# The 32 sample rows copied into all four partition quadrants, and their hi/lo products stacked into one full-array matmul

## The chip, the cores and the metric

The kernel runs on one core of a Trainium2 chip. The metric is the device time of one execution in microseconds (us). TensorE multiplies; ScalarE and VectorE read its results and prepare its operands; SyncE issues all DMAs.

## The reference

Two layers (DEPTH) are applied to two token streams at once: a prompt of 256 rows and a sample of 32 rows, both of 2048 channels. Every weight is used on both.

```python
def mixer_layer(x, s0, pos, ret_chunk, ...):
    h = rmsnorm(x, norm_g)
    q, k, v, gr, u, vm, gm, ar, am = jnp.split(h @ w_in, _split_points(), axis=-1)
    q, k = rotary(q, pos), rotary(k, pos) * (DK ** -0.5)
    o, s_new = retention(q, k, v, s0, ret_chunk)      # 8 heads, DK=128, DV=256
    r_branch = (silu(gr) * head_groupnorm(o)) @ w_ret_out
    vn = layernorm(gelu(vm), ln_g, ln_b)
    m = gelu(u) * (ws_masked @ vn + bias)             # per group of 256 channels, over positions
    m_branch = (silu(gm) * m) @ w_mlp_out
    merged = sigmoid(ar) * r_branch + sigmoid(am) * m_branch
    return x + merged @ w_o, s_new, vn
# retention, the sample as one chunk of 32 rows:
#   out = (q k^T * decay) v + (q * q_dec) s0 ;  s_new = gamma^32 s0 + (k * k_dec)^T v
```

Outputs are the two streams after a last rmsnorm, the retention states of both, and vn of the sample.

## The kernel before

Activations stand transposed, channels on partitions, and 288 columns are tokens: 256 of the prompt (TP), then 32 of the sample (TS). A large projection is a job: one pair of output tiles of 128 channels, over 2048 channels of input in four pieces. In a piece TensorE does 4 x 2 blocks of three products (`mm3`) of 128x128 weights with 288 columns into `ps`. Three, because a float32 value is split in two: `to_hi` (ScalarE, cast to the type float32r) and `to_lo` (VectorE, value minus its hi part). A product is then hi*hi + hi*lo + lo*hi. A product over a contraction of the 32 sample rows uses a quarter of TensorE's rows.

The main loop goes through the pieces in the order of the job list: vm, then u and gm alternately, am with the gMLP projection, then per pair of heads q, k, v, gr, v, gr, then ar, the retention projection and the output projection. In each step it emits the weight split of later pieces (hi four ahead, lo three ahead), the weight's DMA seven ahead, the 24 products of this piece, and then `tick()`, which lets every evacuation in progress run up to its next `yield`. So an evacuation's instructions stand on every engine between two pieces, and a `yield` puts one piece of large products between its parts. All engines work in the order in which they were given instructions, and TensorE's order is fixed here.

The places that the change touches, all in evacuations:

- `tok_blocks` (L196) turns a tile of 128 channels x 288 tokens into tokens on partitions: four transposes of prompt blocks (L201), two of the 32 sample columns (L204). `evac_vm` (16 times in all), `evac_k` (8) and `evac_v` (16) call it, one piece after the tile was scaled by VectorE.
- `sgu_gen` (L247) normalises a group of 256 channels and multiplies by the position matrix `ws`. The prompt uses hi and lo (L285, L286), the sample one plain float32 product over 32 rows, once for each half of the channels (L287).
- `evac_k` (L369) makes the decayed keys `kdh`, `kdl`, the scores and their hi and lo parts: `wh`, `wl` for the prompt, `wsh`, `wsl` (tiles w2h, w2l of 32 partitions) for the sample, and `qdh`, `qdl` for the decayed queries. The sample's scores are one plain float32 product (L395).
- `evac_v` (L412) makes v's parts `vh`, `vl`, the output products into `po` (prompt) and `pq` (sample), their group norm, the normalised output `on`, and the new states.
- `evac_gr` (L467) transposes `on` back to channels (L478) and gates it.

Of the kernel before, what the change touches and what calls it, by code (L numbers as in the profile page):

```python
# [42 lines left out]
def trunk(ctx: ExitStack, tc: tile.TileContext, a, o):  # L43
# [29 lines left out]
    wsh = [st([TS, P], f"w2h{i}", F32R) for i in range(2)]  # L73
    wsl = [st([TS, P], f"w2l{i}", F32R) for i in range(2)]
# [29 lines left out]
    def to_hi(src, hi):  # L104
        S.copy(out=hi, in_=src)  # L105
# [90 lines left out]
    def tok_blocks(z):  # L196
        """PE transposes of a [128 ch, 2, T] tile: [tok, 2 blocks, 256] and [32, 256]."""
        p0, p1 = aux(), aux()
        for b in range(2):
            for jj in range(2):  # L200
                PE.transpose(p0[:, b * 256 + jj * 128:b * 256 + jj * 128 + 128],  # L201
                             z[:, jj, b * 128:b * 128 + 128], ident)
        for jj in range(2):
            PE.transpose(p1[0:TS, jj * 128:jj * 128 + 128], z[:, jj, TP:T], ident)  # L204
        return p0.rearrange("p (b c) -> p b c", b=2), p1[0:TS, 0:256]

# [1 line left out]
    def evac_vm(l, c, ps):  # L208
        if "rs" in state:
            z = scaled(ps)  # L210
        else:
# [4 lines left out]
            V.tensor_tensor(out=z, in0=z, in1=bc2(state["rs"]), op=ALU.mult)
        if state.get("vml") != l:
            state["vml"] = l
            state["vmt"] = st([P, 3, DM], "vmacc")
            state["bst"] = st([P, 3, NPR, 6], "bst")  # L220
        vmt, bst = state["vmt"], state["bst"]
        yield
        p0, p1 = tok_blocks(z)
        sl = slice(c * 256, c * 256 + 256)
        S.activation(out=vmt[:, 0:2, sl], in_=p0, func=AF.Gelu)
        S.activation(out=vmt[0:TS, 2, sl], in_=p1, func=AF.Gelu)
        yield
        for b, n in TOK:
            V.bn_stats(out=bst[0:n, b, c], in_=vmt[0:n, b, sl])
        if c == NPR - 1:  # L230
            for b, n in TOK:
                V.bn_aggr(out=mvl[0:n, b], in_=bst[0:n, b].rearrange("p a s -> p (a s)"))
            state["ln"] = rsqrt(mvl[:, :, 1], 3, "ln")

    def load_sgu(l, g):
        if g == NPR:
            return
        lg, lb = st([P, 384], "c0", bufs=2)[:, 0:256], st([P, 256], "c1", bufs=2)
# [6 lines left out]
        state["sgu", g] = (lg, lb, bs, wr)  # L245

    def sgu_gen(l, g):  # L247
        if g == 0:
            load_sgu(l, 0)
        lg, lb, bs, wr = state.pop(("sgu", g))  # L250
# [19 lines left out]
        vh, vl = st([P, 3, 256], "vh", F32R, bufs=2), st([P, 3, 256], "vl", F32R, bufs=2)  # L270
        to_hi(vmt[:, 0:2, sl], vh[:, 0:2])
# [3 lines left out]
        to_lo(vmt[:, 0:2, sl], vh[:, 0:2], vl[:, 0:2])  # L275
# [5 lines left out]
        for d in range(2):  # L281
            p = aux().rearrange("p (b h i) -> p b h i", b=2, h=2)
            ds = slice(d * 128, d * 128 + 128)
            for b in range(2):
                PE.matmul(p[:, b], vh[:, b, ds], w2, start=True, stop=False)  # L285
                PE.matmul(p[:, b, 0], vl[:, b, ds], w2[:, 0], start=False, stop=True)  # L286
            PE.matmul(ps_[:, d * TS:d * TS + TS], vmt[0:TS, 2, g * 256 + d * 128:g * 256 + d * 128 + 128],  # L287
                      wr[0:TS, 0:TS], start=True, stop=True)
# [80 lines left out]
    def evac_k(l, hp, ps):  # L369
        yield from rotary(ps, "rk", "k")  # L370
        r, rh, rl = state["k"]
        q, qh, ql = state["q"]
        yield
        p0, p1 = tok_blocks(r)
        kh, kl = st([P, 3, 256], "kdh", F32R), st([P, 3, 256], "kdl", F32R)
        parts = []
        for b, n in TOK:
            for jj in range(2):
                cs = slice(jj * 128, jj * 128 + 128)
                parts.append((p0[:, b, cs] if b < 2 else p1[:, cs], kdec[0:n, 2 * hp + jj, b:b + 1],  # L380
                              kh[0:n, b, cs], kl[0:n, b, cs]))
# [7 lines left out]
        for jj in range(2):
# [5 lines left out]
            PE.matmul(p2[0:TS, 0:TS], r[:, jj, TP:T], q[:, jj, TP:T], start=True, stop=True)  # L395
# [16 lines left out]
    def evac_v(l, h, ps):  # L412
        z = scaled(ps)
        s0 = state.pop(("s0", h))
# [3 lines left out]
        p0, p1 = tok_blocks(z)  # L418
        vh, vl = st([P, 3, 256], "vh", F32R, bufs=2), st([P, 3, 256], "vl", F32R, bufs=2)
        parts = ((s0, s0h, s0l), (p0, vh[:, 0:2], vl[:, 0:2]), (p1, vh[0:TS, 2], vl[0:TS, 2]))  # L420
        for src, hi, lo in parts[1:]:
            to_hi(src, hi)
# [13 lines left out]
        mm3(pq[:, 0:256], wsh[jj], wsl[jj], vh[0:TS, 2], vl[0:TS, 2], stop=False)  # L436
# [12 lines left out]
        on = st([P, 3, 256], "on")  # L449
        for b, n in TOK:  # L450
            S.activation(out=on[0:n, b], in_=src[b][0:n], func=AF.Identity,  # L451
                         bias=nb[0:n, b:b + 1], scale=y[0:n, b:b + 1])
# [4 lines left out]
        mm3(p[:, 256:512], kh[0:TS, 2, cs], kl[0:TS, 2, cs], vh[0:TS, 2], vl[0:TS, 2])  # L457
# [9 lines left out]
    def evac_gr(l, h, ps):  # L467
# [5 lines left out]
        on = state.pop(("on", h))  # L473
        for e in range(2):
            p = aux()
            es = slice(e * 128, e * 128 + 128)
            for b, n in TOK:
                PE.transpose(p[:, b * P:b * P + n], on[0:n, b, es], ident[0:n, 0:n])  # L478
            V.tensor_tensor(out=z[:, e], in0=z[:, e], in1=p[:, 0:T], op=ALU.mult)
# [285 lines left out]
def _consts():  # L765
# [83 lines left out]
```

## Time and profile before

| | |
|---|---|
| median of 3 runs | 2424.78 us (2424.29 to 2424.97) |
| span of the profiled execution, first to last instruction | 2423.4 us |
| median less that span (start and end of an execution) | 1.4 us |
| TensorE busy, matmul instructions | 2408.4 us, 99%, 18004 |
| VectorE busy | 1368.0 us, 56% |
| ScalarE busy | 998.3 us, 41% |
| mean granted TensorE clock | 0.997 |

An execution's time is a little longer than the span that its profile shows, so the profiled execution's own time is taken as its span and 1.4 us around it. In the profile's rows L12 is line 12 of the kernel before, PE is TensorE's products, PEld its weight loads, DVE VectorE and ACT ScalarE; out<-in names the tiles. A product's record starts where the product starts; its end is modelled, and records of successive products overlap. What a product costs is thus the distance from its start to the next one's. `32*128` in a row means that 32 rows and 128 columns of TensorE's array are used.

### The profile page before, as it was taken

How to read it: one execution, taken by the hardware profiler on the slowest of the kernel's cores; microseconds unless marked ns; L12 is line 12 of the kernel's file. 1: busy time of each engine (PE TensorE's matmuls, PEld its weight loads, DVE VectorE, ACT ScalarE, POOL GpSimd, SP SyncE). 2: the span in 40 equal slices, each digit the busy share in tenths (PEclk: the TensorE clock that was granted, in tenths of full speed). 3: DMA queues.
4: the chain of work that ended last, by engine and by line, in shares of the span. 5: the costliest groups of instructions: out<-in, count | busy, mean ns of one | idle time of the engine just before them, and what ended most of it. 6: DMA issues, size and time to landing. Idle time of an engine off the chain costs nothing.

```text
span 2423.4 us, 42844 instructions
## 1 busy us (share of the span) xinstructions
PE 2408.4 (99%) x18004; PEld 2384.7 (98%) x18004; DVE 1368.0 (56%) x1999; ACT 998.3 (41%) x1245; POOL 0.2 (0%) x4
## 2 busy tenths in 40 slices
PE   9999999999999999999999999999999999999997
PEld 9999999999999999999999999999999999999997
DVE  7476654446666664455555666544466566544544
ACT  6345443334344343334433445433344344433342
POOL 0000000000000000000000000000000000000000
PEclk9999999999999999999999999999999999999998
DMA  6455544454544544455645555444544444445553
GB/s 239 155 175 171 184 157 166 165 164 158 168 137 159 165 138 167 165 166 192 210 162 156 185 170 169 163 165 165 170 152 158 153 150 158 144 162 167 166 193 117
DMA packets 127825, 401.78 MB, mean 166 GB/s; under 512 B 14736, under 2 KB 32400, under 8 KB 127632
## 3 DMA queue, kind: packets, MB, share of 16 engines
q1 hardware_dynamic: 127632, 399.04, 50.4%
q8 instruction: 141, 2.31, 0.4%
q14 instruction: 52, 0.43, 0.1%
HBM read 389.55 MB, written 9.44 MB: 165 GB/s over the span
## 4 chain that ended last, share of the span: by engine, by line
PE 99%; DVE 0%; DMA 0%; SPq 0%; ACT 0%; issue 0%; DVEq 0%
PE ps L111 31%; PE ps L112 31%; PE ps L113 31%; PE aux L111 1%; PE aux L113 1%; PE aux L112 1%; PE aux L201 1%; PE aux L478 1%; PE aux L285 1%; PE aux L287 0%; PE aux L204 0%; DMA raw<-in_w_in 0%; DVE vmacc L758 0%; PE aux L286 0%; SPq L78 0%; PE aux L165 0%
## 5 line engine op out<-in xcount | busy, mean ns | idle before, releaser
L108 DVE TENSOR_TENSOR wlo<-raw,whi 128x1024 fp32r<-128x1024 f32 (+1 forms) x705 | 859.5, 1220 | 601.4 <-PE ps L113 374.6
L105 ACT CAST whi<-raw 128x1024 fp32r<-128x1024 f32 (+1 forms) x705 | 734.9, 1047 | 839.8 <-PE ps L112 695.0
L111 PE MATMUL ps<-Ah,whi 128*128 128x288 f32 x2816 | 836.8, 297 | 0.5 <-ACT whi L105 0.5
L113 PE MATMUL ps<-Ah,wlo 128*128 128x288 f32 x2816 | 831.0, 295 | 1.3 <-DVE wlo L108 1.3
L112 PE MATMUL ps<-Al,whi 128*128 128x288 f32 x2816 | 830.0, 295 | 0.0
L111 PE MATMUL ps<-Bh,whi 128*128 128x288 f32 x2784 | 826.1, 297 | 0.0
L113 PE MATMUL ps<-Bh,wlo 128*128 128x288 f32 x2784 | 824.2, 296 | 0.0
L112 PE MATMUL ps<-Bl,whi 128*128 128x288 f32 x2784 | 823.8, 296 | 0.0
L111 PEld LDWEIGHTS ps<-Ah,whi 128*128 128x128 f32 x2816 | 528.8, 188 | 3.1 <-ACT whi L105 0.9
L113 PEld LDWEIGHTS ps<-Ah,wlo 128*128 128x128 f32 x2816 | 528.7, 188 | 2.3 <-DVE wlo L108 2.3
L112 PEld LDWEIGHTS ps<-Al,whi 128*128 128x128 f32 x2816 | 528.5, 188 | 0.0
L111 PEld LDWEIGHTS ps<-Bh,whi 128*128 128x128 f32 x2784 | 523.0, 188 | 2.1
L112 PEld LDWEIGHTS ps<-Bl,whi 128*128 128x128 f32 x2784 | 524.0, 188 | 0.0
L113 PEld LDWEIGHTS ps<-Bh,wlo 128*128 128x128 f32 x2784 | 522.5, 188 | 0.0
L193 DVE TENSOR_TENSOR z<-ps,rsb 128x576 f32<-128x576 f32 x81 | 61.1, 755 | 108.2 <-PE ps L113 108.2
L451 ACT ACTIVATE on<-aux,gnb,gny 128x256 f32<-128x256 f32 (+1 forms) x48 | 23.3, 554 | 71.6 <-DVE gnb L447 71.6
L442 DVE BATCH_NORM_STATS2 gst<-aux 128x6 f32<-128x256 f32 x48 | 19.1, 427 | 52.9 <-PE aux L113 52.9
L290 DVE TENSOR_TENSOR rqh<-aux,wh 128x256 f32<-128x256 f32 x32 | 13.6, 425 | 34.9 <-PE aux L286 34.0
L317 ACT ACTIVATE z<-z 128x576 f32<-128x576 f32 x16 | 11.0, 686 | 46.3 <-DVE z L193 46.3
L193 DVE TENSOR_TENSOR zu<-ps,rsb 128x576 f32<-128x576 f32 x20 | 15.1, 756 | 25.6 <-PE ps L113 25.6
L343 DVE TENSOR_TENSOR zu<-ps,cosr 128x576 f32<-128x576 f32 x16 | 12.1, 758 | 30.6 <-PE ps L113 30.6
L334 DVE TENSOR_TENSOR vmacc<-ps,z 128x576 f32<-128x576 f32 x16 | 12.1, 758 | 30.6 <-PE ps L113 30.6
(221 smaller groups left out, 1171.1 us busy)
## 6 DMA issues: line engine op xcount, KB each, us to landing
raw<-in_w_in SPq DMA_DIRECT2D x511, 512.0 KB, 4.6
raw<-in_w_mlp SPq DMA_DIRECT2D x64, 512.0 KB, 4.6
raw<-in_w_ret SPq DMA_DIRECT2D x64, 512.0 KB, 4.6
raw<-in_w_o SPq DMA_DIRECT2D x64, 512.0 KB, 4.5
c<-in_dmask SPq DMA_DIRECT2D x16, 192.0 KB, 4.8
vmacc<-in_x SPq DMA_DIRECT2D x8, 288.0 KB, 7.5
wh<-in_ws_b SPq DMA_DIRECT2D x16, 144.0 KB, 6.4
zu<-in_x SPq DMA_DIRECT2D x8, 288.0 KB, 3.0
```

The source lines that it names most:

```text
L105: S.copy(out=hi, in_=src)
L108: V.tensor_tensor(out=lo, in0=src, in1=hi.bitcast(F32), op=ALU.subtract)
L111: PE.matmul(out, lh, rh, start=start, stop=False)
L112: PE.matmul(out, lh, rl, start=False, stop=False)
L113: PE.matmul(out, ll, rh, start=False, stop=stop)
L193: V.tensor_tensor(out=z, in0=ps[:, :, 0:T], in1=bc2(state["rs"]), op=ALU.mult)
L201: PE.transpose(p0[:, b * 256 + jj * 128:b * 256 + jj * 128 + 128], z[:, jj, b * 128:b * 128 + 128], ident)
L285: PE.matmul(p[:, b], vh[:, b, ds], w2, start=True, stop=False)
L290: V.tensor_tensor(out=x, in0=p[:, :, 1], in1=bs[:, 0:TP].rearrange("p (b i) -> p b i", b=2), op=ALU.add)
L442: V.bn_stats(out=bst[:, b], in_=src[b])
L451: S.activation(out=on[0:n, b], in_=src[b][0:n], func=AF.Identity, bias=nb[0:n, b:b + 1], scale=y[0:n, b:b + 1])
L478: PE.transpose(p[:, b * P:b * P + n], on[0:n, b, es], ident[0:n, 0:n])
```

## The change

The 32 sample columns are copied four times side by side by a new ScalarE copy, `fourfold` (tile `z4`), and a transpose of 128 such columns leaves the sample rows in all four partition quadrants. The stationary and the moving operand of a sample product then hold, quadrant by quadrant, different halves: one has (hi, hi, lo, lo), the other (hi, lo, hi, lo). One product over 128 rows sums hi*hi + hi*lo + lo*hi + lo*lo. `HALF` and `ODD` are the quadrants in which VectorE replaces hi by lo, in place.

So: the three sample products into `pq` become one with `w2s`; the three of the sample state become one with `kh`, `vh`; the gate's plain float32 product becomes one float32r product with `wsk`, made from a new input `ws_s` (the corner of ws four times over, 16 KB a group, 16 more loads); the scores (L395) and the two sample transposes (L204) get 128 columns of weights instead of 32; the six back transposes become five, since the two sample halves are written to two quadrants of a tile `ons` by ScalarE and transposed at once. Elementwise work on the sample goes over 128 partitions instead of 32.

```diff
+    def fourfold(x):
+        z4 = st([P, 2, P], "z4", bufs=2)
+        S.copy(out=z4.rearrange("p j (r t) -> p j r t", r=4),
+               in_=x[:, :, TP:T].unsqueeze(2).to_broadcast([P, 2, 4, TS]))
+        return z4
 # tok_blocks
-            PE.transpose(p1[0:TS, jj * 128:jj * 128 + 128], z[:, jj, TP:T], ident)
+            PE.transpose(p1[:, jj * 128:jj * 128 + 128], z4[:, jj], ident)
 # evac_vm (evac_k and evac_v alike)
+        z4 = fourfold(z)
         yield
-        p0, p1 = tok_blocks(z)
+        p0, p1 = tok_blocks(z, z4)
 # sgu_gen
+        wsk = st([P, TS], "wsk", F32R, bufs=2)
+        to_hi(wq, wsk)
...
+                for q in ODD:
+                    to_lo(wq[q], wsk[q], wsk[q])
...
-        to_hi(vmt[:, 0:2, sl], vh[:, 0:2])
+        to_hi(vmt[:, :, sl], vh)
...
+        to_lo(vmt[HALF, 2, sl], vh[HALF, 2], vh[HALF, 2])
...
-            PE.matmul(ps_[:, d * TS:d * TS + TS], vmt[0:TS, 2, g * 256 + d * 128:g * 256 + d * 128 + 128],
-                      wr[0:TS, 0:TS], start=True, stop=True)
+            PE.matmul(ps_[:, d * TS:d * TS + TS], vh[:, 2, ds], wsk, start=True, stop=True)
 # evac_k
+        r4 = fourfold(r)
...
-            PE.matmul(p2[0:TS, 0:TS], r[:, jj, TP:T], q[:, jj, TP:T], start=True, stop=True)
+            PE.matmul(p2[:, 0:TS], r4[:, jj], q[:, jj, TP:T], start=True, stop=True)
 # evac_v
-        for src, hi, lo in parts:
-            to_lo(src, hi, lo)
+        to_lo(s0, s0h, s0l)
+        to_lo(p0, vh[:, 0:2], vl)
+        for q in ODD:
+            to_lo(p1[q], vh[q, 2], vh[q, 2])
...
-        mm3(pq[:, 0:256], wsh[jj], wsl[jj], vh[0:TS, 2], vl[0:TS, 2], stop=False)
+        PE.matmul(pq[:, 0:256], w2s[jj], vh[:, 2], start=True, stop=False)
...
+        for e in range(2):
+            S.activation(out=ons[e * TS:e * TS + TS], in_=pq[0:TS, e * 128:e * 128 + 128], func=AF.Identity,
+                         bias=nb[0:TS, 2:3], scale=y[0:TS, 2:3])
...
-        mm3(p[:, 256:512], kh[0:TS, 2, cs], kl[0:TS, 2, cs], vh[0:TS, 2], vl[0:TS, 2])
+        PE.matmul(p[:, 256:512], kh[:, 2, cs], vh[:, 2], start=True, stop=True)
 # evac_gr
-                PE.transpose(p[:, b * P:b * P + n], on[0:n, b, es], ident[0:n, 0:n])
+                PE.transpose(p[e][:, b * P:b * P + P], on[:, b, e * 128:e * 128 + 128], ident)
+            if e == 0:
+                PE.transpose(p[0][:, TP:TP + P], ons, ident)
```

On TensorE, the end of one head's output products, before (wh, wl scores of the prompt, w2h, w2l of the sample, qdh, qdl decayed queries, vh, vl values, s0h, s0l the old state; a number behind a name tells buffers apart):

```order
L111 MATMUL aux<-vh,wh 128x256
L112 MATMUL aux<-vl,wh 128x256
L113 MATMUL aux<-vh,wl 128x256
L111 MATMUL aux<-vh,w2h_82 128x256
L112 MATMUL aux<-vl,w2h_82 128x256
L113 MATMUL aux<-vh,w2l_84 128x256
L111 MATMUL aux<-s0h,qdh_78 128x256
L112 MATMUL aux<-s0l,qdh_78 128x256
L113 MATMUL aux<-s0h,qdl_80 128x256
```

and after:

```order
L111 MATMUL aux<-vh,wh 128x256
L112 MATMUL aux<-vl,wh 128x256
L113 MATMUL aux<-vh,wl 128x256
L461 MATMUL aux<-vh,w2s_82 128x256
L111 MATMUL aux<-s0h,qdh_78 128x256
L112 MATMUL aux<-s0l,qdh_78 128x256
L113 MATMUL aux<-s0h,qdl_80 128x256
```

Three rows became one and the rest keeps its place; the whole of TensorE's list shrinks from 17715 rows to 17635.

On ScalarE, from the keys' evacuation to a head's values (kdh decayed keys, zu the rotated keys), before:

```order
L383 ACTIVATE kdh<-aux,kdec 128x128 x4
L383 ACTIVATE kdh<-aux,kdec 32x128 x2
L105 CAST whi<-raw 128x1024
L105 CAST wh<-z 128x384
L105 CAST w2h_82<-z 32x32
L105 CAST qdh_78<-z 128x32
L105 CAST s0h<-c_5717 128x256
L105 CAST whi<-raw 128x1024
```

and after:

```order
L122 COPY z_6109<-zu 128x256
L105 CAST whi<-raw 128x1024
L402 ACTIVATE kdh<-aux,kdec 128x128 x6
L105 CAST whi<-raw 128x1024
L105 CAST wh<-z 128x384
L105 CAST qdh_78<-z 128x32
L105 CAST w2s_82<-z 128x32
L122 COPY z_6213<-z 128x256
L105 CAST s0h<-c_5787 128x256
L105 CAST whi<-raw 128x1024
```

The two COPY rows are fourfold copies (z_6109 and z_6213 are tiles z4); each stands ahead of a weight cast of a later piece.

More of the change, by code (lines that the diff above doesn't have):

```diff
@@ L72, in trunk @@
     qdl = [st([P, P], f"qdl{i}", F32R) for i in range(2)]
-    wsh = [st([TS, P], f"w2h{i}", F32R) for i in range(2)]
-    wsl = [st([TS, P], f"w2l{i}", F32R) for i in range(2)]
+    w2s = [st([P, P], f"w2s{i}", F32R) for i in range(2)]
+    ons = st([P, P], "ons")
     mvl = st([P, 3, 2], "mvl")
@@ L113, in mm3 @@
         PE.matmul(out, ll, rh, start=False, stop=stop)
+    HALF = slice(64, 128)
+    ODD = (slice(32, 64), slice(96, 128))
+    def fourfold(x):
[3 more added lines that the diff above has]
+        return z4
     class Set:
@@ L194, in scaled, with tok_blocks @@
         return z
-    def tok_blocks(z):
+    def tok_blocks(z, z4):
         p0, p1 = aux(), aux()
@@ L203, in tok_blocks @@
         for jj in range(2):
-            PE.transpose(p1[0:TS, jj * 128:jj * 128 + 128], z[:, jj, TP:T], ident)
-        return p0.rearrange("p (b c) -> p b c", b=2), p1[0:TS, 0:256]
+            PE.transpose(p1[:, jj * 128:jj * 128 + 128], z4[:, jj], ident)
+        return p0.rearrange("p (b c) -> p b c", b=2), p1[:, 0:256]
     def evac_vm(l, c, ps):
@@ L221, in evac_vm @@
         vmt, bst = state["vmt"], state["bst"]
+        z4 = fourfold(z)
         yield
-        p0, p1 = tok_blocks(z)
+        p0, p1 = tok_blocks(z, z4)
         sl = slice(c * 256, c * 256 + 256)
         S.activation(out=vmt[:, 0:2, sl], in_=p0, func=AF.Gelu)
-        S.activation(out=vmt[0:TS, 2, sl], in_=p1, func=AF.Gelu)
+        S.activation(out=vmt[:, 2, sl], in_=p1, func=AF.Gelu)
         yield
-        for b, n in TOK:
-            V.bn_stats(out=bst[0:n, b, c], in_=vmt[0:n, b, sl])
+        for b in range(3):
+            V.bn_stats(out=bst[:, b, c], in_=vmt[:, b, sl])
         if c == NPR - 1:
-            for b, n in TOK:
-                V.bn_aggr(out=mvl[0:n, b], in_=bst[0:n, b].rearrange("p a s -> p (a s)"))
+            for b in range(3):
+                V.bn_aggr(out=mvl[:, b], in_=bst[:, b].rearrange("p a s -> p (a s)"))
             state["ln"] = rsqrt(mvl[:, :, 1], 3, "ln")
@@ L237, in load_sgu @@
             return
-        lg, lb = st([P, 384], "c0", bufs=2)[:, 0:256], st([P, 256], "c1", bufs=2)
+        lg, lb = st([P, 416], "c0", bufs=2)[:, 0:256], st([P, 256], "c1", bufs=2)
         load(lg, a["ln_g"][l, g].partition_broadcast(P))
@@ L244, in load_sgu @@
         load(wr, a["ws"][l, g])
-        state["sgu", g] = (lg, lb, bs, wr)
+        wq = st([P, TS], "wsq", bufs=2)
+        load(wq, a["ws_s"][l, g])
+        state["sgu", g] = (lg, lb, bs, wr, wq)
     def sgu_gen(l, g):
@@ L249, in sgu_gen @@
             load_sgu(l, 0)
-        lg, lb, bs, wr = state.pop(("sgu", g))
+        lg, lb, bs, wr, wq = state.pop(("sgu", g))
         while "ln" not in state:
@@ L258, in sgu_gen @@
         to_hi(wr, w2[:, 0])
+        wsk = st([P, TS], "wsk", F32R, bufs=2)
+        to_hi(wq, wsk)
         sl = slice(g * 256, g * 256 + 256)
-        for b, n in TOK:
-            x = vmt[0:n, b, sl]
-            V.scalar_tensor_tensor(out=x, in0=x, scalar=mvl[0:n, b, 0:1], in1=lg[0:n],
+        for b in range(3):
+            x = vmt[:, b, sl]
+            V.scalar_tensor_tensor(out=x, in0=x, scalar=mvl[:, b, 0:1], in1=lg,
                                    op0=ALU.subtract, op1=ALU.mult)
-            V.scalar_tensor_tensor(out=x, in0=x, scalar=r[0:n, b:b + 1], in1=lb[0:n],
+            V.scalar_tensor_tensor(out=x, in0=x, scalar=r[:, b:b + 1], in1=lb,
                                    op0=ALU.mult, op1=ALU.add)
@@ L268, in sgu_gen @@
                 to_lo(wr, w2[:, 0], w2[:, 1])
+                for q in ODD:
+                    to_lo(wq[q], wsk[q], wsk[q])
         yield
[L270 to L271 removed]
+        vh, vl = st([P, 3, 256], "vh", F32R, bufs=2), st([P, 2, 256], "vl", F32R, bufs=2)
+        to_hi(vmt[:, :, sl], vh)
         load(o["gv"][l, :, sl], vmt[0:TS, 2, sl])
@@ L274, in sgu_gen @@
         yield
-        to_lo(vmt[:, 0:2, sl], vh[:, 0:2], vl[:, 0:2])
+        to_lo(vmt[:, 0:2, sl], vh[:, 0:2], vl)
+        to_lo(vmt[HALF, 2, sl], vh[HALF, 2], vh[HALF, 2])
         yield
@@ L358, in pre_q @@
         for h in (2 * hp, 2 * hp + 1):
-            d = st([P, 384], "c0", bufs=2)
+            d = st([P, 416], "c0", bufs=2)
             load(d, a["dmask"][h])
@@ L372, in evac_k @@
         q, qh, ql = state["q"]
+        r4 = fourfold(r)
         yield
-        p0, p1 = tok_blocks(r)
-        kh, kl = st([P, 3, 256], "kdh", F32R), st([P, 3, 256], "kdl", F32R)
+        p0, p1 = tok_blocks(r, r4)
+        kh, kl = st([P, 3, 256], "kdh", F32R), st([P, 2, 256], "kdl", F32R)
         parts = []
-        for b, n in TOK:
+        for b in range(3):
             for jj in range(2):
                 cs = slice(jj * 128, jj * 128 + 128)
-                parts.append((p0[:, b, cs] if b < 2 else p1[:, cs], kdec[0:n, 2 * hp + jj, b:b + 1],
-                              kh[0:n, b, cs], kl[0:n, b, cs]))
+                src, dc, hi = p0[:, b, cs] if b < 2 else p1[:, cs], kdec[:, 2 * hp + jj, b:b + 1], kh[:, b, cs]
+                parts.append((src, dc, hi, kl[:, b, cs] if b < 2 else None))
         for src, dc, hi, lo in parts:
@@ L385, in evac_k @@
         for src, dc, hi, lo in parts:
+            if lo is None:
+                src, dc, hi = src[HALF], dc[HALF], hi[HALF]
+                lo = hi
             V.scalar_tensor_tensor(out=lo, in0=src, scalar=dc, in1=hi.bitcast(F32),
@@ L394, in evac_k @@
             mm3(p[:, 256:384], rh[:, jj, j1], rl[:, jj, j1], qh[:, jj, j1], ql[:, jj, j1])
-            PE.matmul(p2[0:TS, 0:TS], r[:, jj, TP:T], q[:, jj, TP:T], start=True, stop=True)
+            PE.matmul(p2[:, 0:TS], r4[:, jj], q[:, jj, TP:T], start=True, stop=True)
             d = state.pop(("d", h))
             w = st([P, 2 * T], "z", bufs=3)
-            V.tensor_tensor(out=w[:, 0:384], in0=p[:, 0:384], in1=d, op=ALU.mult)
-            V.tensor_tensor(out=w[0:TS, 384:416], in0=p2[0:TS, 0:TS], in1=d[0:TS, 0:TS], op=ALU.mult)
+            V.tensor_tensor(out=w[:, 0:384], in0=p[:, 0:384], in1=d[:, 0:384], op=ALU.mult)
+            V.tensor_tensor(out=w[:, 384:416], in0=p2[:, 0:TS], in1=d[:, 384:416], op=ALU.mult)
             V.tensor_tensor(out=w[:, 416:448], in0=q[:, jj, TP:T], in1=qdec[:, h], op=ALU.mult)
             wh, wl = st([P, 384], "wh", F32R, bufs=2), st([P, 384], "wl", F32R, bufs=2)
-            parts = ((w[:, 0:384], wh, wl),
-                     (w[0:TS, 384:416], wsh[jj][:, 0:TS], wsl[jj][:, 0:TS]),
-                     (w[:, 416:448], qdh[jj][:, 0:TS], qdl[jj][:, 0:TS]))
-            for src, hi, lo in parts:
+            w2 = w2s[jj][:, 0:TS]
+            parts = ((w[:, 0:384], wh, wl), (w[:, 416:448], qdh[jj][:, 0:TS], qdl[jj][:, 0:TS]),
+                     (w[HALF, 384:416], w2[HALF], w2[HALF]))
+            for src, hi, lo in parts[:2]:
                 to_hi(src, hi)
+            to_hi(w[:, 384:416], w2)
             yield
@@ L413, in evac_v @@
         z = scaled(ps)
+        z4 = fourfold(z)
         s0 = state.pop(("s0", h))
@@ L417, in evac_v @@
         yield
[L418 to L422, printed above, removed]
+        p0, p1 = tok_blocks(z, z4)
+        vh, vl = st([P, 3, 256], "vh", F32R, bufs=2), st([P, 2, 256], "vl", F32R, bufs=2)
+        to_hi(p0, vh[:, 0:2])
+        to_hi(p1, vh[:, 2])
         yield
-        for src, hi, lo in parts:
-            to_lo(src, hi, lo)
+        to_lo(s0, s0h, s0l)
+        to_lo(p0, vh[:, 0:2], vl)
+        for q in ODD:
+            to_lo(p1[q], vh[q, 2], vh[q, 2])
         yield
@@ L448, in evac_v @@
         yield
[L449 to L452, printed above, removed]
+        on = st([P, 2, 256], "on")
+        for b in range(2):
+            S.activation(out=on[:, b], in_=src[b], func=AF.Identity, bias=nb[:, b:b + 1], scale=y[:, b:b + 1])
+        for e in range(2):
+            S.activation(out=ons[e * TS:e * TS + TS], in_=pq[0:TS, e * 128:e * 128 + 128], func=AF.Identity,
+                         bias=nb[0:TS, 2:3], scale=y[0:TS, 2:3])
         cs = slice(jj * 128, jj * 128 + 128)
@@ L473, in evac_gr @@
         on = state.pop(("on", h))
+        p = [aux(), aux()]
         for e in range(2):
[L475 to L479, printed above, removed]
+            for b in range(2):
+                PE.transpose(p[e][:, b * P:b * P + P], on[:, b, e * 128:e * 128 + 128], ident)
+            if e == 0:
+                PE.transpose(p[0][:, TP:TP + P], ons, ident)
+        V.tensor_tensor(out=z[:, 0], in0=z[:, 0], in1=p[0][:, 0:T], op=ALU.mult)
+        V.tensor_tensor(out=z[:, 1, 0:TP], in0=z[:, 1, 0:TP], in1=p[1][:, 0:TP], op=ALU.mult)
+        V.tensor_tensor(out=z[:, 1, TP:T], in0=z[:, 1, TP:T], in1=p[0][:, T:T + TS], op=ALU.mult)
         hi, lo = state["rg"].alloc(h)
@@ L667, in trunk @@
         S.copy(out=q, in_=zero)
-    for q in wsh + wsl:
-        S.copy(out=q, in_=zero[0:TS])
+    for q in w2s:
+        S.copy(out=q, in_=zero)
+    S.copy(out=ons, in_=zero)
     prep0(0)
@@ L781, in _consts @@
         kd[:, :, b] = g[None, :] ** (TP - 1 - (p + b * P)) * sc
-    kd[:TS, :, 2] = g[None, :] ** (TS - 1 - p[:TS]) * sc
-    d = np.concatenate([d, d[:, :, :P]], -1)
+    kd[:, :, 2] = g[None, :] ** (TS - 1 - p % TS) * sc
+    d = np.concatenate([d, d[:, :, :P], np.tile(d[:, :TS, :TS], (1, P // TS, 1))], -1)
     qd = g[None, :, None] ** (np.arange(TS)[None, None, :] + 1.0)
@@ L819 @@
         "ws": cc(x["ws"].transpose(0, 1, 3, 2)),
+        "ws_s": cc(np.tile(x["ws"].transpose(0, 1, 3, 2)[:, :, :TS, :TS], (1, 1, P // TS, 1))),
         "ws_b": cc(np.concatenate([wsb, wsb, wsb[:, :, :TS]], -1)),
```

## The prediction

> **What bounds the kernel now.** I read the page first, then the waits of TensorE (PE), then TensorE's own timeline around the places that the change touches, and last the groups of instructions for counts and for the prices of the added work. From the page: the span, TensorE's share, and the chain that ended last, by engine.
>
> ```profile
> span 2423.4 us, 42844 instructions
> PE 2408.4 (99%) x18004; PEld 2384.7 (98%) x18004; DVE 1368.0 (56%) x1999; ACT 998.3 (41%) x1245; POOL 0.2 (0%) x4
> PE 99%; DVE 0%; DMA 0%; SPq 0%; ACT 0%; issue 0%; DVEq 0%
> ```
>
> The chain is TensorE from one end to the other. A busy share cannot say whether it waits inside, so the waits (engine, line, releaser: us in total, times, longest):
>
> ```profile
> PE aux L173 <- DVE z L98: 2.8, 1, 2.8
> PE ps L113 <- DVE wlo L108: 1.3, 4, 0.7
> ```
>
> These are the two longest totals. TensorE stands still for hardly 6 us outside the start and the tail; 2.8 of them lie in the tail. So the time is the sum of the distances between the starts of successive matmuls, and an edit is worth what it does to those distances. VectorE (56%) and ScalarE (41%) count only where TensorE would have to wait for them.
>
> **The matmuls that change, and their number** (group, out<-in, rows*columns of the array, shape, count | busy, mean ns):
>
> ```profile
> L111 PE MATMUL aux<-vh,w2h 32*128 32x256 f32 x16 | 6.1, 383 | 0.0
> L111 PE MATMUL aux<-vh,kdh 32*128 32x256 f32 x16 | 6.1, 383 | 0.0
> L478 PE MATMUL aux<-ident,on 32*128 32x32 f32 x32 | 7.8, 243 | 0.0
> L287 PE MATMUL aux<-wsr,vmacc 32*128 32x32 f32 x64 | 12.9, 282 | 0.0
> L395 PE MATMUL aux<-zu 128*32 128x32 f32 x32 | 4.0, 207 | 0.0
> ```
>
> Sixteen heads (8 in each layer) and sixteen spatial-gate groups. A plain float32 matmul leaves two records, so L287 is 2 matmuls a group and L395 one a head. The means overlap and are no price; starts are. TensorE's timeline at one head's output products (start, length):
>
> ```profile
> 591.75 0.28 PE L111 MATMUL aux<-vh,wh 128*128 128x256 f32 x1
> ...
> 592.70 0.28 PE L113 MATMUL aux<-vh,wl 128*128 128x256 f32 x1
> 592.91 0.38 PE L111 MATMUL aux<-vh,w2h 32*128 32x256 f32 x1
> ...
> 593.45 0.39 PE L111 MATMUL aux<-s0h,qdh 128*128 128x256 f32 x1
> 593.68 0.28 PE L112 MATMUL aux<-s0l,qdh 128*128 128x256 f32 x1
> ```
>
> Eight distances from 591.75 to 592.70: 0.119 us each for a full-array product of 256 columns. The first 32-row product starts 0.21 after its predecessor, and s0h, the first full-array one after it, keeps 0.23 instead of 0.119: about 0.09 and 0.11 are lost where the used part of the array changes, with operands long there. From 592.70 to 593.68 there are 0.98; with one full-array product there are three ordinary distances, 0.357. **Saved: 0.62 x 16 = 10.0 us.**
>
> The same head's state product, where the large projection (ps) follows:
>
> ```profile
> 597.69 0.28 PE L113 MATMUL aux<-vh,kdl 128*128 128x256 f32 x1
> 597.90 0.38 PE L111 MATMUL aux<-vh,kdh 32*128 32x256 f32 x1
> ...
> 598.45 0.40 PE L111 MATMUL ps<-Ah,whi 128*128 128x288 f32 x1
> 598.69 0.30 PE L112 MATMUL ps<-Al,whi 128*128 128x288 f32 x1
> ```
>
> 597.69 to 598.69 is 1.00; after it is 0.119 + 0.119 + 0.13 (a ps distance, next fence) = 0.37. **Saved: 0.63 x 16 = 10.1 us.**
>
> The transposes back (six before, five after, none of 32 rows):
>
> ```profile
> 601.74 1.10 PE L478 MATMUL aux<-ident,on 128*128 128x128 f32 x6
> ...
> 603.01 0.29 PE L112 MATMUL ps<-Al,whi 128*128 128x288 f32 x1
> 603.14 0.29 PE L113 MATMUL ps<-Ah,wlo 128*128 128x288 f32 x1
> ```
>
> 601.74 to 603.01 is 1.27. A full transpose keeps 0.11 (two L201 from 51.81 to 52.03, further down), so after: 5 x 0.11 + 0.13 = 0.68. **Saved: 0.59 x 16 = 9.4 us.**
>
> The spatial gate (ten logical products; L287's two become single-pass):
>
> ```profile
> 136.52 0.28 PE L285 MATMUL aux<-wsp,vh 128*128 128x256 f32 x1
> ...
> 136.87 0.22 PE L286 MATMUL aux<-wsp,vl 128*128 128x128 f32 x1
> ...
> 138.53 0.29 PE L112 MATMUL ps<-Al,whi 128*128 128x288 f32 x1
> ```
>
> Three distances to 136.87 make 0.117 each, and the whole stretch is 2.01. A full-array product with 32 moving columns doesn't exist in the trace. Its nearest relation is the one-column product against the 128x128 operand in the statistics (the chain of waits, six in 0.67):
>
> ```profile
> 1219.82 0.67 PE aux L165 x6
> ```
>
> that is 0.112, although it streams one column: the weight load sets it. I take 0.112. After: 8 x 0.117 + 2 x 0.112 + 0.13 = 1.29. **Saved: 0.72 x 16 = 11.5 us.** Ends: two at 0.06 would save 1.6 us more in all; two at 0.23, what the first product after a change keeps, 3.8 less.
>
> The sample scores (L395) become 128 columns wide:
>
> ```profile
> 580.09 0.27 PE L113 MATMUL aux<-rqh,rkl 128*128 128x128 f32 x1
> ...
> 580.71 0.29 PE L112 MATMUL ps<-Al,whi 128*128 128x288 f32 x1
> ```
>
> 0.62 before. After: three load-set distances of 0.112 and one of 0.13, 0.47. **Saved: 0.15 x 16 = 2.4 us** (between nothing and 0.26 each, if the two records kept 0.06).
>
> **Transposes of the sample rows, now 128 wide (L204, 80 of them): nothing.**
>
> ```profile
> 51.81 0.38 PE L201 MATMUL aux<-ident,z 128*128 128x128 f32 x2
> 52.03 0.38 PE L204 MATMUL aux<-ident,z 128*32 128x128 f32 x2
> 52.24 0.60 PE L201 MATMUL aux<-ident,z 128*128 128x128 f32 x4
> ```
>
> Two L201 take 0.22 and two L204 0.21: the narrow ones are no cheaper where full ones follow. Their weight loads do differ, and that is a rival below:
>
> ```profile
> L204 PEld LDWEIGHTS aux<-ident,z 128*32 128x32 f32 x64 | 6.2, 97 | 0.4
> L201 PEld LDWEIGHTS aux<-ident,z 128*128 128x128 f32 x128 | 15.1, 140 | 0.3
> ```
>
> The Trainium skill's page "TensorE: Matmul & The Clock Gate", section "LDWEIGHTS (loading the stationary operand)", speaks against the change here: it makes load time proportional to the columns at 1.2 per ns, so 96 more columns would be an estimated 0.08 us more, 6.4 us over 80. By that rule the sum would be 37.0; the pair at 52.03 shows no such gain for narrow loads today.
>
> **Work added on engines beside the path, costed at nothing, and its cover.** Prices from these groups:
>
> ```profile
> L105 ACT CAST s0h<-c 128x256 fp32r<-128x256 f32 x16 | 6.4, 400 | 0.0
> L108 DVE TENSOR_TENSOR vl<-aux,vh 32x256 fp32r<-32x256 f32 x16 | 6.4, 402 | 0.0
> L108 DVE TENSOR_TENSOR w2l<-z,w2h 32x32 fp32r<-32x32 f32 x16 | 2.8, 173 | 0.0
> ```
>
> ScalarE: 40 fourfold copies x 0.40 = 16 us (the source is read four times over, which no row shows; 0.40 is the same output size), with some 0.5 us a head or group for the wider cast, the new cast of ws_s and the split of "on", about 8: 25 us in all, 41% to 42%. VectorE: a second low part in each evac_v (0.40), three in each gate group (0.17 + 0.17 + 0.40), a third product in evac_gr (0.17): 1.31 x 16 = 21 us, 56% to 57%. Widening an operation from 32 to 128 partitions is free, since the cost goes by columns: the rows above show 0.40 at 32 and at 128 partitions with 256 columns.
>
> What is queued behind them: the copy waits on ScalarE for VectorE's scaled tile, and the weight cast of a later piece stands behind it; TensorE waits for the copy at the next transposes. One such case, with VectorE's timeline, then TensorE's:
>
> ```profile
> 581.07 0.74 DVE L193 TENSOR_TENSOR z<-ps,rsb 128x576 f32<-128x576 f32 x1
> ...
> 587.41 1.00 DVE L108 TENSOR_TENSOR vl<-aux,vh 128x512 fp32r<-128x512 f32 x2
> ```
>
> ```profile
> 584.66 0.66 PE L201 MATMUL aux<-ident,z 128*128 128x128 f32 x4
> ```
>
> The scaled tile ends at 581.81 and its transposes come at 584.66: 2.85 us for a copy of 0.4. The low parts end at 588.41 and their products come at 591.75: 3.3 us for 0.4 more. The thin place is the first gate group of each layer:
>
> ```profile
> 135.47 0.68 DVE L108 TENSOR_TENSOR vl<-vmacc,vh 128x512 fp32r<-128x512 f32 x1
> ```
>
> It ends at 136.15, 0.37 before the group's first product and 0.83 before its sample product, and 0.75 is added ahead of that: covered by a hair, or twice half a microsecond late. If the cover went everywhere, each late microsecond would cost TensorE 40. The 16 new DMAs (ws_s, 16 KB) and the dmask rows longer by 32 columns go through SyncE's queue, ahead of weight loads; TensorE waits for no DMA in the list above, and casts run four pieces ahead, so nothing. At the start three constant copies replace four on ScalarE, ahead of the first weight cast; that cast waits for its DMA.
>
> **Sum.** 10.0 + 10.1 + 9.4 + 11.5 + 2.4 = 43.4. The profiled span, 2423.4, becomes 2380.0; the median of the runs, 2424.78, stands 1.4 over that span (start and end of the execution), which I keep: 2381.4.
>
> **Rivals.**
> A, wide loads show: 80 loads longer by 140 - 97 ns make 3.5 us dearer, 2385. Against it stands the equal pair at 52.03; for it, that the narrow load is shorter and something must hide it.
> B, the lost 0.2 us at each 32-row group isn't a change of array shape but the small products' own lateness, and stays with whatever comes in their place. Then only distances of removed instructions go: 64 x 0.119, 16 x 0.11 and 32 x 0.112, 13 us, 2412. Against it: the first full-array product afterwards is late too, and in the gate that comes twice a group.
> C, slower: ScalarE takes the fourfold copy so late that TensorE, strictly in order, stops at the transposes of all 40 tiles. It decides from 1.1 us a tile (43.4/40), so the copy must end 3.9 us after its tile in the case above. A copy held until the piece after (24 products of 0.13, 3.1 us later than its cover) would cost 40 x 3.1 = 124, 2505. For it: ScalarE is in order. Against it: ScalarE is 59% idle and only a cast of 1.05 us or so can be between.
> D, part of that: the first gate groups and a few others wait, 5 to 10 us together, 2386 to 2391.
>
> **Chances.** Forecast 70% (its own range 2378 to 2385), A 12%, D 9%, B 4%, C 3%, larger gains 2%. The range takes the forecast's ends (two 32-column products and L395 cheaper, 2378; the dear end of the gate products, 2385), A and D: 2377 to 2391. From no change a measurement here tells 0.2%, 4.8 us: all but C are faster by more, 97%; of C 1% lies near its point of 1.1 us and so within, 2% slower.
>
> **What would show it.** The page after should have TensorE at 17892 products (64 + 16 + 32 fewer), no group with 32 rows or 32 columns of the array, and no distance over 0.14 where one stood. The chain stays 99% TensorE. ScalarE near 1023 us, VectorE near 1389. Wrong would be: distances of 0.2 before the w2s, kdh or ons products (B), transposes at more than 0.11 (A), TensorE waits on a z4 copy or on the gate's low part (C, D).

## The result and the profile after

The changed kernel takes 2382.17 us (median of 4 runs, 2381.86 to 2383.48) against 2424.88 for the kernel before on the same chip: 42.7 us less, a ratio of 0.982 (0.981 to 0.984). 2381.4 was forecast. From the page of the kernel after, the span and the engines:

```profile
span 2380.3 us, 42818 instructions
PE 2365.4 (99%) x17892; PEld 2363.9 (99%) x17892; DVE 1389.3 (58%) x2079; ACT 1025.5 (43%) x1316; POOL 0.2 (0%) x4
```

TensorE has 112 product records less and is still 99% busy; its busy time fell by 43.0 us, the span by 43.1. The added work is about what was expected, 21 us on VectorE and 27 on ScalarE (25 was forecast), and no wait came of it. TensorE's waits after:

```profile
PE aux L184 <- DVE z L98: 2.8, 1, 2.8
PE aux L681 <- DVE ones L675: 1.0, 1, 1.0
PE ps L111 <- ACT whi L105: 1.0, 2, 0.6
PE ps L113 <- DVE wlo L108: 0.8, 3, 0.4
```

L184 is the statistics at the tail, L681 the warm-up at the start. None of the changed products is in the list.

The five stretches, in TensorE's timeline after, at the places that the prediction showed. Output products (w2s is the stacked one), then state product (L484) up to the large projection:

```profile
586.29 0.28 PE L113 MATMUL aux<-vh,wl 128*128 128x256 f32 x1
586.41 0.28 PE L461 MATMUL aux<-vh,w2s 128*128 128x256 f32 x1
586.53 0.28 PE L111 MATMUL aux<-s0h,qdh 128*128 128x256 f32 x1
586.64 0.28 PE L112 MATMUL aux<-s0l,qdh 128*128 128x256 f32 x1
...
590.66 0.28 PE L113 MATMUL aux<-vh,kdl 128*128 128x256 f32 x1
590.78 0.28 PE L484 MATMUL aux<-vh,kdh 128*128 128x256 f32 x1
590.90 0.29 PE L111 MATMUL ps<-Ah,whi 128*128 128x288 f32 x1
591.03 0.29 PE L112 MATMUL ps<-Al,whi 128*128 128x288 f32 x1
```

586.29 to 586.64 is 0.35, where 0.98 stood; 590.66 to 591.03 is 0.37, where 1.00 stood. Each saves 0.63, 10.1 us over 16 heads, and every distance in these rows is an ordinary one. The back transposes and the gate:

```profile
594.08 0.38 PE L504 MATMUL aux<-ident,on 128*128 128x128 f32 x2
...
594.76 0.29 PE L112 MATMUL ps<-Al,whi 128*128 128x288 f32 x1
```

```profile
136.16 0.28 PE L304 MATMUL aux<-wsp,vh 128*128 128x256 f32 x1
...
136.57 0.23 PE L306 MATMUL aux<-wsk,vh 128*128 128x32 f32 x1
...
137.44 0.29 PE L112 MATMUL ps<-Al,whi 128*128 128x288 f32 x1
```

0.68 instead of 1.27 (9.4 us over 16), and 1.28 instead of 2.01 (11.7 us). The scores:

```profile
573.71 0.22 PE L111 MATMUL aux<-rqh,rkh 128*128 128x128 f32 x1
573.77 0.28 PE L112 MATMUL aux<-rql,rkh 128*128 128x128 f32 x1
573.89 0.27 PE L113 MATMUL aux<-rqh,rkl 128*128 128x128 f32 x1
574.00 0.36 PE L417 MATMUL aux<-zu,z 128*128 128x32 f32 x2
574.19 0.38 PE L111 MATMUL ps<-Ah,whi 128*128 128x288 f32 x1
574.40 0.29 PE L112 MATMUL ps<-Al,whi 128*128 128x288 f32 x1
```

573.89 to 574.40 is 0.51 instead of 0.62: 1.8 us. The five make 43.1 us, the whole difference of the spans. These are one place each, times 16; averaged over all places of each kind in the two traces they are 9.8, 10.0, 9.3, 11.8 and 1.7 us, together 42.7. So the agreement to a tenth is luck of rounding, and 0.4 us lie elsewhere.

### The profile page after: what moved, and what is told of

It reads as the page before. It is cut to its first block, busy times and chain, and to the rows that moved or that the text cites. A ratio compares the mean times of both kernels' runs of the same rounds, so it can differ in the third digit from the quotient of the medians.

```text
span 2380.3 us, 42818 instructions
## 1 busy us (share of the span) xinstructions
PE 2365.4 (99%) x17892; PEld 2363.9 (99%) x17892; DVE 1389.3 (58%) x2079; ACT 1025.5 (43%) x1316; POOL 0.2 (0%) x4
## 4 chain that ended last, share of the span: by engine, by line
PE 99%; DVE 0%; DMA 0%; SPq 0%; ACT 0%; issue 0%; DVEq 0%
PE ps L113 31%; PE ps L112 31%; PE ps L111 31%; PE aux L112 1%; PE aux L113 1%; PE aux L111 1%; PE aux L212 1%; PE aux L304 0%; PE aux L215 0%; PE aux L504 0%; DMA raw<-in_w_in 0%; DVE vmacc L789 0%; PE aux L305 0%; PE aux L417 0%; PE aux L176 0%; PE aux L306 0%
## 5 line engine op out<-in xcount | busy, mean ns | idle before, releaser
L112 PE MATMUL ps<-Al,whi 128*128 128x288 f32 x2816 | 830.5, 295 | 0.0
L112 PE MATMUL ps<-Bl,whi 128*128 128x288 f32 x2784 | 823.7, 296 | 0.0
L112 PEld LDWEIGHTS ps<-Al,whi 128*128 128x128 f32 x2816 | 528.7, 188 | 0.0
L112 PEld LDWEIGHTS ps<-Bl,whi 128*128 128x128 f32 x2784 | 524.0, 188 | 0.0
L204 DVE TENSOR_TENSOR z<-ps,rsb 128x576 f32<-128x576 f32 x81 | 61.2, 755 | 107.9 <-PE ps L113 107.9
L476 ACT ACTIVATE on<-aux,gnb,gny 128x256 f32<-128x256 f32 x32 | 16.3, 561 | 64.4 <-DVE gnb L472 64.4
L122 ACT COPY z<-z 128x256 f32<-128x256 f32 x32 | 13.0, 407 | 63.7 <-DVE z L204 59.5
```

The source lines that it names most:

```text
L112: PE.matmul(out, lh, rl, start=False, stop=False)
L122: S.copy(out=z4.rearrange("p j (r t) -> p j r t", r=4), in_=x[:, :, TP:T].unsqueeze(2).to_broadcast([P, 2, 4, TS]))
L204: V.tensor_tensor(out=z, in0=ps[:, :, 0:T], in1=bc2(state["rs"]), op=ALU.mult)
L476: S.activation(out=on[:, b], in_=src[b], func=AF.Identity, bias=nb[:, b:b + 1], scale=y[:, b:b + 1])
```

## The experiments

Theory S, the prediction's: time is lost where the used rows of TensorE's array change. Rival N: small products are late in themselves, so that their number is what counts. All times below are medians; after was 2382.17, and 2382.40 in a second set of runs. The sets ran on different chips; the kernel before, run in each set, took 2424.88 to 2425.22 us.

**The number without the shape.** Edit of after:

```diff
-        PE.matmul(pq[:, 0:256], w2s[jj], vh[:, 2], start=True, stop=False)
+        for n in range(3):
+            PE.matmul(pq[:, 0:256], w2s[jj], vh[:, 2], start=(n == 0), stop=False)
 # and the state product alike
```

> The stacked sample products (into pq and into the sample state) are issued three times each, over all 128 rows; the sample's output and state come out tripled. It restores the number of products of before without their 32 rows. Theory S (the time lay where the used rows of the array change): 4 more products a head x 16 heads x 0.118 = 7.6 us, 2389.8. Rival N (each product over the sample's rows costs what it cost before, 0.245 = (0.62 + 0.119)/3): 64 x 0.245 = 15.7, 2398.

Measured: 2389.95 us (2388.78 to 2391.06), 7.8 more than after. The timeline shows the three at ordinary distances:

```profile
586.84 0.52 PE L462 MATMUL aux<-vh,w2s 128*128 128x256 f32 x3
587.19 0.28 PE L111 MATMUL aux<-s0h,qdh 128*128 128x256 f32 x1
```

0.35 for three, with all 128 rows. N is out, and theory S holds so far: more products add ordinary distances only.

**The shape without the number: 32 rows, then 64.**

```diff
-        PE.matmul(pq[:, 0:256], w2s[jj], vh[:, 2], start=True, stop=False)
+        PE.matmul(pq[:, 0:256], w2s[jj][0:TS], vh[0:TS, 2], start=True, stop=False)   # or 0:64
 # and the state product alike
```

> After, with the two stacked sample products of a head run over the first 32 rows only (leaves out the terms with a low part). The number of products is that of after, only the used rows differ. Theory S: each of 32 products starts 0.09 late and makes its successor 0.11 late, 32 x 0.20 = 6.4 us, 2388.6, with distances of 0.21 and 0.22 around w2s and kdh. Rival N (their number was the cost): 2382, distances of 0.118.

> The same with 64 rows (leaves out the terms lo*hi and lo*lo). Theory S in its wide form (any change of the used rows): 6.4 us as with 32 rows, 2388.6. If only 32 rows are late: 2382. If lateness grows with the rows left out: between, 2385 to 2387.

Measured: 2394.73 us with 32 rows (2394.56 to 2395.03) and 2394.54 with 64 (2394.01 to 2394.77): 12.5 more than after, twice what was expected, and the same for both. TensorE's products with 32 rows, and its weight loads there:

```profile
586.52 0.28 PE L113 MATMUL aux<-vh,wl 128*128 128x256 f32 x1
586.73 0.38 PE L461 MATMUL aux<-vh,w2s 32*128 32x256 f32 x1
587.04 0.38 PE L111 MATMUL aux<-s0h,qdh 128*128 128x256 f32 x1
587.26 0.28 PE L112 MATMUL aux<-s0l,qdh 128*128 128x256 f32 x1
```

```profile
586.73 0.18 PEld L461 LDWEIGHTS aux<-vh,w2s 32*128 32x128 f32 x1
587.04 0.19 PEld L111 LDWEIGHTS aux<-s0h,qdh 128*128 128x128 f32 x1
587.15 0.19 PEld L112 LDWEIGHTS aux<-s0l,qdh 128*128 128x128 f32 x1
```

s0l's load starts 0.11 ahead of its product, as all ordinary ones do. The loads of w2s and of s0h start with their products: at a change the next weights aren't loaded beside the product before. So one change costs twice: 0.09 by which the first product is late, and 0.10 to 0.11 by which it holds up its successor. The expectation counted these two once a product. But there are two changes, into the small rows and out again: 0.74 from 586.52 to 587.26 against 0.35, that is 0.39 a product, 0.195 a change, and 32 x 0.39 = 12.5.

Is it the change that pays, or each product with few rows? The kernel before answers that, with three such products in a row. Between the rows that the prediction shows, its trace has

```profile
593.13 0.27 PE L112 MATMUL aux<-vl,w2h 32*128 32x256 f32 x1
593.25 0.28 PE L113 MATMUL aux<-vh,w2l 32*128 32x256 f32 x1
```

so the distances from 592.70 on are 0.21, 0.22, 0.12, 0.20 and 0.23: late at both ends, ordinary between two small products. In all 0.98 against five ordinary distances, 0.39 for three small products as for one. It is the change. With 64 rows:

```profile
586.78 0.28 PE L113 MATMUL aux<-vh,wl 128*128 128x256 f32 x1
586.99 0.38 PE L461 MATMUL aux<-vh,w2s 64*128 64x256 f32 x1
587.30 0.38 PE L111 MATMUL aux<-s0h,qdh 128*128 128x256 f32 x1
587.52 0.28 PE L112 MATMUL aux<-s0l,qdh 128*128 128x256 f32 x1
```

0.74 again: with 64 rows a change pays what it pays with 32. The Trainium skill's page "TensorEngine Tiling (Array Packing)", section "Key Properties", says that a change of tiling mode drains TensorE. The late starts at a change of rows fit that; a drain itself can't be seen in these traces, where products' ends are modelled. What these runs add is the size, 0.195 us a change, over half of it the weight load that stands bare.

**The gate's product, shape and pass apart.**

```diff
-            PE.matmul(ps_[:, d * TS:d * TS + TS], vh[:, 2, ds], wsk, start=True, stop=True)
+            PE.matmul(ps_[:, d * TS:d * TS + TS], vh[0:TS, 2, ds], wsk[0:TS], start=True, stop=True)
```

> After, with the gate's sample product run over the first 32 rows, still in one float32r pass (leaves out the terms with a low part). Of the 11.8 us that the gate's stretch lost, theory S gives 32 x 0.20 = 6.4 to the change of rows, so 2388.6, and the rest to the second pass of the plain float32 product. Rival: all of it was the second pass and the time stays at 2382.

Measured: 2390.56 us (2390.21 to 2391.18), 8.4 more than after. In the timeline:

```profile
137.65 0.28 PE L304 MATMUL aux<-wsp,vh 128*128 128x256 f32 x1
...
138.15 0.28 PE L306 MATMUL aux<-wsk,vh 32*128 32x32 f32 x1
138.35 0.38 PE L304 MATMUL aux<-wsp,vh 128*128 128x256 f32 x1
...
139.41 0.29 PE L112 MATMUL ps<-Al,whi 128*128 128x288 f32 x1
```

From 137.65 to L112 is 1.76, against 1.28 after: 0.48 for two products in the group, 0.24 each, less than the 0.39 in the run with 32 rows. The back transposes of before come to the same: their 1.27 is 0.48 above six full transposes and a ps distance (6 x 0.11 + 0.13), for two products of 32 rows that stand apart. Why two changes cost less in these places no run tests; perhaps part of the bare load takes the place of a wait for weights that was there anyway. Of the 11.7 us that the gate gained, then, some 8 are the shape, and the rest is about what the second records of the plain float32 products cost (32 at 0.112, 3.6).

**Columns instead of rows.** An added product of 32 columns and all rows, overwritten by the full one:

```diff
+        PE.matmul(p[0:TS, 256:512], kh[:, 2, jj * 128:jj * 128 + TS], vh[:, 2], start=True, stop=True)
         PE.matmul(p[:, 256:512], kh[:, 2, cs], vh[:, 2], start=True, stop=True)
```

> After, with one more product a head ahead of the sample's state product: the same rows, but 32 columns of the array (its result is overwritten by the full product). If a change of the used columns costs what a change of rows does (0.195 each by the runs with 32 and 64 rows, two changes): 16 x (0.118 + 0.39) = 8.1 us, 2390.3. If columns are free, as the narrow transposes suggest: 16 x 0.118 = 1.9, 2384.1.

Measured: 2385.25 us (2384.47 to 2386.47), 3.1 more than after.

```profile
591.44 0.28 PE L484 MATMUL aux<-vh,kdh 128*32 128x256 f32 x1
591.56 0.28 PE L485 MATMUL aux<-vh,kdh 128*128 128x256 f32 x1
591.68 0.29 PE L111 MATMUL ps<-Ah,whi 128*128 128x288 f32 x1
```

0.12 and 0.12: no change is paid, and 16 x 0.118 is 1.9 us, near the 2.4 by which this run's span is longer (2382.7). The rest of the 3.1 isn't TensorE's: two of the four runs spent 2.9 and 3.2 us outside their span, where 1.8 is usual. Narrow columns of a float32r product are free. In plain float32 they are not:

```diff
+            PE.matmul(p2[0:TS, 0:TS], r4[:, jj, 0:TS], q[:, jj, TP:T], start=True, stop=True)
             PE.matmul(p2[:, 0:TS], r4[:, jj], q[:, jj, TP:T], start=True, stop=True)
```

> After, with the sample's scores computed once more ahead of the wide product: plain float32 again, but 32 columns of the array, into the same place. In the run with a 32-column float32r product columns were free (0.116 a product). If columns are free for plain float32 too: 2 records x 0.112 x 16 = 3.6 us, 2385.8. If the late start of 0.09 that the kernel before shows ahead of L395 belongs to narrow columns in plain float32: two changes of 0.195 more a head, 16 x 0.61 = 9.8 us, 2392.

Measured: 2387.54 us (2387.18 to 2388.17), 5.1 more than after in the same set of runs, between the two.

```profile
574.41 0.27 PE L113 MATMUL aux<-rqh,rkl 128*128 128x128 f32 x1
574.62 0.25 PE L417 MATMUL aux<-zu,z 128*32 128x32 f32 x2
574.80 0.41 PE L418 MATMUL aux<-zu,z 128*128 128x32 f32 x2
```

L417 starts 0.21 after its predecessor, as L395 did before, where the wide one kept 0.11. A late start there is, but a head pays 5.1/16 = 0.32 for two records, 0.22 by their loads, and only 0.10 for the changes. That is also what the kernel before lost around L395, 0.11 a head by the stretches. Why plain float32 differs from float32r here wasn't tried further.

**One part alone: wide sample transposes.** The kernel before with this edit (and one buffer for `z4`, where after has two):

```diff
+        z4 = fourfold(z)                      # in evac_vm, evac_k, evac_v
-            PE.transpose(p1[0:TS, jj * 128:jj * 128 + 128], z[:, jj, TP:T], ident)
+            PE.transpose(p1[:, jj * 128:jj * 128 + 128], z4[:, jj], ident)
```

> The kernel before with one part of the change alone: the fourfold copies, and the sample's transposes 128 columns wide from them (their result is used from the first 32 rows as before). Prediction's own term: nothing, 2425. Rival A (wide weight loads show): 80 x (140 - 97 ns) = 3.5 us, 2428.5. That ScalarE's copies are not covered would show here too, as waits of the transposes on them.

Measured: 2425.58 us (2425.02 to 2427.05) against 2425.14 for the kernel before in the same set, ratio 1.000 (0.999 to 1.001). The six transposes of a tile take 0.57 up to the next large product in both traces. The profiled spans are equal too, 2423.4; the 0.4 us more stand outside them. So loads of 128 columns in place of 32 cost nothing here, nor do 40 ScalarE copies, and rival A is out: its 3.5 us lie beyond the interval.

**How much cover the copies have.** `fourfold` copies eight times over:

```diff
+        for _ in range(8):
-        S.copy(out=z4...)
+            S.copy(out=z4...)
```

> After, with each fourfold copy issued eight times over, to measure the cover of rival C. In the trace of after the copy ends 1.79 us ahead of its transposes in the spatial gate's tiles and in every second head's values, 2.2 in the other heads' and 3.0 in the keys'. Seven more copies at 0.31 (distance from a copy to the next instruction) end 2.2 later: about 22 tiles wait 0.4 us, 9 us in all, 2391. If the cover is elastic (later work catches up) it stays under that; if ScalarE's other work suffers (weight casts late), over 2400.

Measured: 2411.30 us (2410.07 to 2411.71), 29 more than after. The waits of TensorE, its timeline at one tile, and ScalarE's there:

```profile
PE aux L216 <- ACT z L123: 18.7, 29, 1.5
PE aux L213 <- ACT vmacc L238: 2.6, 1, 2.6
```

```profile
85.17 0.60 PE L213 MATMUL aux<-ident,z 128*128 128x128 f32 x4
86.50 0.44 PE L216 MATMUL aux<-ident,z 128*128 128x128 f32 x2 [0.73 <-ACT z L123]
```

```profile
82.97 3.47 ACT L123 COPY z<-z 128x256 f32<-128x256 f32 x8 [3.05 <-DVE z L205]
```

The copies follow each other at 0.44; the 0.31 of the expectation was the distance from a copy to another instruction, and whether it matters that the eight copies write one tile, no run tells. So seven more are 3.1 us. The cover was mis-read too: 1.79 is the time to the first of a tile's six transposes, and the two that need the copy come behind four others, 2.2 us after it. 3.1 overruns 2.2 by 0.9, and so the trace has it: the late end 86.44 meets transposes that could have started at 85.6. Added up over all tiles, the stretches of their transposes grew by 27.9 of the 28.2 us by which the span did: 19 tiles lose 0.95 each, eight with 2.7 us of cover 0.47, the eight of the keys with 3.5 nothing, and three at the start of the two layers 6.2 together, 2.8 of it at the tile that waits for vmacc. So late weight casts, the expectation's way to over 2400, are not the cause. Rival C is real as a mechanism, then, and even copies that end 3 us later don't reach its point, the time of the kernel before.

**A version that follows from it.** If a transpose costs 0.109 whatever its width, two narrow ones should be one. For evac_vm and evac_v (evac_k keeps its two):

```diff
+    def twofold(x):                           # columns: half 0 twice, half 1 twice
+        z4 = st([P, P], "z4", bufs=2)
+        S.copy(out=z4.rearrange("p (j r t) -> p j r t", j=2, r=2),
+               in_=x[:, :, TP:T].unsqueeze(2).to_broadcast([P, 2, 2, TS]))
+        return z4
...
+            PE.transpose(p1[:, 0:128], z4, ident)
...
-        S.activation(out=vmt[:, 2, sl], in_=p1, func=AF.Gelu)
+        for hf in (slice(0, 64), HALF):
+            for jj in range(2):
+                S.activation(out=vmt[hf, 2, c * 256 + jj * 128:c * 256 + jj * 128 + 128],
+                             in_=p1[jj * 64:jj * 64 + 64, 0:128], func=AF.Gelu)
 # hi and lo parts in evac_v in quarters alike
```

> After, with both channel halves of the sample transposed at once in the 32 tiles of evac_vm and evac_v (two copies of each half side by side, so one transpose instead of two), and ScalarE and VectorE writing the quadrants in quarters from it. TensorE does 32 transposes less at 0.109: 3.5 us, 2378.7. Rival: three more ScalarE operations a tile, about 0.9 us later, reach the values' low parts and so TensorE: 2382 or slower. In the trace of before the low parts had 3.3 us, so I expect the gain.

> The version with one sample transpose instead of two in 32 tiles, beside the kernel after on the same chip: 2.5 to 3.5 us faster than it (its span was 2.7 us shorter, its stretches 3.5), 2379.

> The kernel after, unchanged, beside the packed version on the same chip: 2382.

Measured: 2379.64 us (2378.98 to 2380.43), and beside the kernel after on the same chip 2379.30 (2379.17 to 2379.36) against 2382.40 (2382.26 to 2383.35): 3.1 us less, of 2.5 to 3.5 expected. Ratios to before in that set are 0.981 (0.980 to 0.982) and 0.982 (0.981 to 0.984); these intervals overlap, the runs themselves don't, and each tile's stretch is 0.11 shorter. The spans differ by 3.4 (medians 2377.2 and 2380.6); 0.4 is lost again outside them. So it is a little faster than the kernel after.

```profile
66.05 0.60 PE L218 MATMUL aux<-ident,z 128*128 128x128 f32 x4
66.48 0.27 PE L224 MATMUL aux<-ident,z 128*128 128x128 f32 x1
```

One L224 follows the four, and TensorE's waits hold no entry for it: the longer evacuation stayed hidden.

## Why the prediction was right

The main step was right: TensorE's own distances are the time, so that a stretch could be re-laid from the distances of neighbours. Term by term, forecast and measured: outputs 10.0 and 10.1, state 10.1 and 10.1, back transposes 9.4 and 9.4, gate 11.5 and 11.7, scores 2.4 and 1.8, sample transposes 0 and 0 (shown by the run with that part alone). The sum, 43.4, came out at 43.1.

The one mis-sized term is the scores' 0.15 a head, measured 0.11. Its stretch begins in the middle of short products, where the record of a start is early: 573.71 to 573.77 is 0.06, though the weight loads there follow each other at 0.11 to 0.12 throughout, and the difference comes back in the 0.21 from 574.19 to 574.40 where 0.13 is ordinary. The kernel before has the same early record:

```profile
579.98 0.27 PE L112 MATMUL aux<-rql,rkh 128*128 128x128 f32 x1
```

This product starts 0.06 behind the one before it (579.92). So the 0.62 taken from before held that debt, and the 0.47 put in its place did not. Over the whole stretch of a head's scores, from one large product to another, the same prices come out. For the same reason one sign was too strict: distances over 0.14 do stand after (574.19 to 574.40, and 0.22 behind the gate's products and the back transposes), each behind short products and without a change of rows.

The time was forecast 0.8 us short. The span was 0.3 off; the rest is the 1.4 for start and end, taken from a median less the span of one run. Each run after stands about 1.8 above its own span, and so does each run of before in the later sets.

The other step that ran short was a reading, not a term: "about 0.09 and 0.11 are lost where the used part of the array changes" are the two halves of one change, and a group pays two changes. The forecast was safe from it, as it took the whole stretch from the rows; the expectation for 32 rows, built on the piece, was off by half. With it the gain divides: two changes are 0.39 in the outputs and in the state (12.5 us together), some 8 in the gate, and in the back transposes 0.59 less one transpose, 0.48, 7.7 us (worked out from the stretch, not run alone); with the scores' 1.8, a matter of columns in plain float32, that makes 30 us of shape. The other 13 are fewer products, all that rival B would have gained. B, the small products' own lateness, fell with the time itself (2412 forecast), and with the runs that kept the number and changed the shape, and the other way round.

Costed at nothing, and rightly: VectorE's 1389.3 us and ScalarE's 1025.5 met the forecast 1389 and 1023. That an operation costs the same on 32 and on 128 partitions was read from one row of ScalarE and one of VectorE; VectorE's own row before bears it out, 412 ns against the 402 of 32 partitions:

```profile
L108 DVE TENSOR_TENSOR s0l<-c,s0h 128x256 fp32r<-128x256 f32 x16 | 6.6, 412 | 0.0
```

At the first gate group, the thin place of rival D, VectorE's timeline after shows

```profile
135.51 0.42 DVE L108 TENSOR_TENSOR vh<-vmacc,vh 64x256 fp32r<-64x256 f32 x1
```

which ends at 135.93, 0.64 ahead of the product that needs it at 136.57. In the second layer's first group it is 2.0. The copies end at least 2.2 us ahead of their transposes in the trace of after.

## What to carry to other kernels

Where TensorE is 99% busy, read the starts of its products between two undisturbed ones, and re-lay the stretch from distances that stand beside it; busy times and single distances after short products mislead. A small product between full ones costs two changes of the used rows, here 0.39 us among products of 256 columns, more than three times the product itself, and 0.24 in the gate and among the transposes; several small ones in a row share the two. So it pays to fill the rows with something useful, even at the price of copies on an engine with cover. Where a stationary operand is narrow and costs as much as a wide one, ask what else could share it.

## What was not expected of the hardware

A change of used rows costs the same with 64 rows as with 32 (0.195 us each among products of 256 columns), and half of that is a weight load that starts with its product instead of 0.11 ahead. Between two products of the same 32 rows nothing is lost (0.12). Columns behave otherwise: 32 of them are free in a float32r product (0.118) and in a transpose (0.109). In plain float32 a product with 32 columns starts 0.21 after the one before, of which 0.10 a head remained.
